# Five of sixteen expert pairs leave their outputs in DRAM, and the tokens fetch them by index

## The chip, the cores and the metric

The kernel runs on one core of a Trainium2 chip. The metric is device time in microseconds of one execution. TensorE multiplies matrices into PSUM, ScalarE and VectorE work element by element and read PSUM, GpSimd does small work and issues indirect DMAs, SyncE (SP) issues most loads. Each engine runs its instructions in order; DMAs issued from any of them are carried out by 16 DMA engines.

## The reference

One decoder layer on 512 tokens of width 1024, in float32: two attention branches (MLA and MoBA) merged by gates, an output projection, and then a mixture of experts and a final RMSNorm. The change touches the experts alone. In the reference they are

```python
g_sel = argmax(g_logits)                    # one of 4 groups
top_vals, top_idx = top_k(e_in, 2)          # two of the group's 8 experts
weight = p_group * softmax(top_vals)
...
(silu(xb @ w_g[e]) * (xb @ w_u[e])) @ w_d[e]        # e: 32 experts, D 1024, FF 256
out = zeros((T, D)).at[slot_tok].add(ys * slot_w[:, None])
```

Every token goes to two experts, so there are 1,024 choices over 32 experts, and each token's two expert outputs, weighted, are added to its row `x`.

## The kernel before, in words

Up to about 435 us the kernel computes the projections, the attention and the output projection, then the routing. What follows is the experts' stage, `experts()` (L819), which handles two experts at a time in 16 pairs, q = 0 to 15. A pair has 128 slots, one for each partition: 64 for each of its experts. A slot that holds no token has an index outside the tensor, and a gather skips it.

One pair runs so, in the order in which TensorE's instructions are written out (`tc.manual_schedule` for TensorE and GpSimd; the other engines' order is made by the framework's planner, but inside `last()` also by hand):

- `slot_weights` (L733): GpSimd copies the slot's routing weight and norm factor out of the gathered `wg` rows, in three small copies (L738 twice, L739).
- `gate_up` (L760): 32 matmuls G and 32 matmuls U (L769), then ScalarE's silu of G (L774) and VectorE's product with U (L775), both scaled by the norm factor.
- `some(5)`, `act_T`, `some(3)`: the combines of the pair before, with the transposes of the activations (L781) among them. `combine` (L811) adds one 128-token, 512-column block of the pair's outputs to the token rows `x2`: two matmuls (L815, L816) of a one-hot matrix S with the high and the low half of the outputs, and a VectorE add (L817). There are eight for each pair.
- `next_rows`: eight transposes (L746) of the next pair's gathered rows `xg`.
- `gather_rows` (L723) for pair q + 2: GpSimd issues two indirect DMAs (L728), of rows `xg` (4 KB each) and of rows `wg` (132 bytes each).
- `one_hot` (L806): VectorE makes S from the pair's token numbers.
- `down` (L786) for both halves of 512 columns: eight matmuls each (L795), then ScalarE writes the weighted high half (L802) and VectorE the low half (L803).

The weights of pair q + 2 are asked for at the beginning of pair q: six loads of 1 MB (two experts times gate, up and down), all on SP's queue. There are 20 buffers for them (`NH`). Each load also waits until the load before the previous one has landed (`load`, L678), so that two are in flight. The last pair's down weights come in four loads of half the size, by column halves, behind the load of `final_norm`.

After pair 15, `last()` (L876) computes the final norm and stores the output.

Of the kernel before, what the change touches and what calls it, by code (L numbers as in the profile page):

```python
# [10 lines left out]
F32 = mybir.dt.float32  # L11
# [3 lines left out]
I32 = mybir.dt.int32  # L15
U32 = mybir.dt.uint32
AF = mybir.ActivationFunctionType
ALU = mybir.AluOpType
# [3 lines left out]
P = 128  # L22
T = 512
NT = T // P
D = 1024
# [5 lines left out]
NEG = -1e30  # L31
NE = 32
NH = 20


class Layer:
# [351 lines left out]
    def attention(self, br, pairs):  # L388
# [4 lines left out]
        for m in pairs:  # L393
            O = self.op.tile([P, T], F32, name="O", tag="o")
            PT, Es = [], []
            for i in range(NT):
                n = (i + 1) * P
                qs = slice(i * P, n)
                S = both or [self.mp.tile([P, 512], F32, name="S", tag="m") for _ in range(2)]
                for h in range(2):  # L400
# [229 lines left out]
    def route_setup(self):  # L630
        nc, tc, io, c = self.nc, self.tc, self.io, self.const
        self.dram = dp = self.ctx.enter_context(tc.tile_pool(name="dram", bufs=1, space=bass.MemoryType.DRAM))
        self.x2d = dp.tile([T, D], F32, name="x2d")
        self.Wd = dp.tile([T, NE + 1], F32, name="Wd")
        self.wr = c.tile([P, KD, 40], F32, name="wr")
        nc.gpsimd.memset(self.wr, 0.0)
        self.load_late(self.wr[:, :, 0:4], io["w_router_group"][0].rearrange("(j p) g -> p j g", p=P))
        for g in range(4):
            self.load_late(self.wr[:, :, 8 + 8 * g:16 + 8 * g],
                              io["w_router_expert"][0, g].rearrange("(j p) e -> p j e", p=P))  # L640
        self.gpj = c.tile([P, KD], F32, name="gpj")
        self.load_late(self.gpj, io["ffn_norm"][0].rearrange("(p j) -> p j", p=P))
        self.gcol = gcol = c.tile([P, KD], F32, name="gcol")
        self.load_late(gcol, io["ffn_norm"][0].rearrange("(j p) -> p j", p=P))
        nc.vector.tensor_scalar(self.gpj, self.gpj, 32.0, None, ALU.mult)
        nc.vector.tensor_scalar(gcol, gcol, 32.0, None, ALU.mult)
        nc.vector.tensor_tensor(self.wr, self.wr, gcol.unsqueeze(2).to_broadcast([P, KD, 40]), ALU.mult)
        self.rb = c.tile([P, 40], F32, name="rb")
        nc.gpsimd.memset(self.rb, -3e38)
        self.load_late(self.rb[:, 0:4], io["b_router_group"][0:1, :].to_broadcast([P, 4]))  # L650
        self.load_late(self.rb[:, 8:40], io["b_router_expert"].rearrange("o g e -> o (g e)")
                          .to_broadcast([P, 32]))
        self.rc = c.tile([P, 33 + NT], F32, name="rc")
        self.load_late(self.rc, io["rconst"])
        self.iota32 = self.rc[:, 0:32]
        self.slot = self.rc[:, 32:33]
        self.token = self.rc[:, 33:33 + NT]
        self.tri = c.tile([P, 2, P], F16, name="tri")
        self.after(nc.gpsimd.dma_start(self.tri, io["tri"]), self.started)
        self.tm = c.tile([P, T], F16, name="tm")  # L660
        self.after(nc.gpsimd.dma_start(self.tm, io["tm"]), self.started)
        self.M = c.tile([P, NT, NE], F16, name="M")
        self.sq = c.tile([P, 2, NT], F32, name="sq")
        self.W = c.tile([P, NT, NE + 1], F32, name="W")
        self.iotaU = c.tile([P, NE], U32, name="iotaU")
        nc.vector.tensor_copy(self.iotaU, self.iota32)


    def new_w(self):
        i = self.nw % NH  # L670
        self.nw += 1
# [139 lines left out]
    def combine(self, S, y, half, t):  # L811
# [4 lines left out]
        nc.tensor.matmul(cp, S[:, t * P:(t + 1) * P], y[1], start=False, stop=True)  # L816
        nc.vector.tensor_tensor(self.x2[t][:, hs], self.x2[t][:, hs], cp, ALU.add)  # L817

    def experts(self):  # L819
        nc, tc = self.nc, self.tc  # L820
        NP = NE // 2
        wgu, wd = {}, {}
        for q in range(3):
            wgu[q], wd[q] = self.load_gu(q), self.load_d(q)
        self.yhl = self.wp.tile([P, 2048], F32R, name="yhl", tag="whi")
        with tc.manual_schedule(engines={mybir.EngineType.PE, mybir.EngineType.Pool}):
            xT, sw, xg = {0: self.xT0}, {}, {}
            S, y, todo = None, None, []
            for q in range(NP):
                if q > 0 and q + 2 < NP:  # L830
                    wgu[q + 2], wd[q + 2] = self.load_gu(q + 2), self.load_d(q + 2)
                    if q + 2 == NP - 1:
                        self.load_final()
                if q:
                    sw[q] = self.slot_weights(q, wg, nc.gpsimd)

                def some(n):
                    for _ in range(min(n, len(todo))):
                        self.combine(S, y[todo[0][0]], *todo[0])
                        todo.pop(0)  # L840

                def between(j):
                    if q == 0 and j == 3:
                        self.tokens()
                        xg[1] = self.gather_rows(self.xi[:, 1:2], self.rows)
                    if q == 0 and j == 5:
                        sw[0] = self.take_weights()
                    if q == 0 and j == 9:
                        self.count_blocks()
                a = self.gate_up(wgu.pop(q), xT.pop(q), lambda: sw[q][1], between)  # L850
                def next_rows():
                    xT[q + 1] = self.new_xT()
                    for g in range(2):
                        self.gathered_T(xg[q + 1][0], xT[q + 1], g)
                if q == 0:
                    next_rows()
                some(5)
                aT = self.act_T(*a)
                some(3)
                if 0 < q < NP - 1:  # L860
                    next_rows()
                if q + 1 < NP:
                    wg = xg.pop(q + 1)[1]
                if q + 2 < NP:
                    xg[q + 2] = self.gather_rows(self.xi[:, q + 2:q + 3])
                S = self.one_hot(self.xf[:, q:q + 1])
                dn = wd.pop(q)
                y = [None, None]
                todo = [(h, t) for h in range(2) for t in range(NT)]
                if q == NP - 1:  # L870
                    self.last(S, dn, aT, sw[q][0])
                    break
                for h in range(2):
                    y[h] = self.down(dn, aT, sw[q][0], h)
# [158 lines left out]
class Route:  # L1033
# [60 lines left out]
    def choose_experts(self):  # L1094
        nc, L = self.nc, self.L
        self.v8, vi = self.tmp("v8", [8]), self.tmp("vi", [8], U32)
        nc.vector.max(self.v8, self.es)
        nc.vector.max_index(vi, self.v8, self.es)
        self.Mk = self.tmp("Mk", [2, NE])
        nc.vector.tensor_tensor(self.Mk, L.iotaU.unsqueeze(1).to_broadcast([P, 2, NE]),  # L1100
                                vi[:, 0:2].unsqueeze(2).to_broadcast([P, 2, NE]), ALU.is_equal)
        nc.vector.tensor_tensor(L.M[:, self.t], self.Mk[:, 0], self.Mk[:, 1], ALU.add)
# [15 lines left out]

    def places(self):
        nc, L, t, N = self.nc, self.L, self.t, self.N  # L1120
        n = self.tmp("n", [2])
        for c in range(2):
            nc.vector.scalar_tensor_tensor(self.es, self.Mk[:, c], 1.0, N, ALU.mult, ALU.mult, accum_out=n[:, c:c + 1])
        self.at(self.AB[:, :, 0:64], n)
# [33 lines left out]
def shape_consts():  # L1158
    out = {}

    def tab(half):
        e = (-np.arange(half, dtype=np.float32) / np.float32(half)).astype(np.float32)
        inv = np.power(np.float32(500000.0), e).astype(np.float32)
        ang = np.arange(T, dtype=np.float32)[:, None] * inv[None, :]
        c, s = np.cos(ang).astype(np.float32), np.sin(ang).astype(np.float32)
        return [c, c, -s, s]
    out["rope"] = np.ascontiguousarray(np.concatenate(tab(16) + tab(8), axis=1))
    q = np.arange(P)[:, None]
    c = np.arange(T)[None, :]
    out["mask"] = np.where(c <= q + 384, np.float32(0), np.float32(NEG)).astype(np.float32)  # L1170
    tri = np.ones((P, 2, P), np.float32)
    tri[:, 0] = np.arange(P)[:, None] <= np.arange(P)[None, :]
    tri[:, 0] += 1024.0 * np.eye(P)
    out["tri"] = tri
    rc = np.zeros((P, 33 + NT), np.float32)
    rc[:, 0:32] = np.arange(32)
    rc[:, 32] = 1025 + np.arange(P) % 64
    rc[:, 33:] = np.arange(P)[:, None] + P * np.arange(NT)[None, :] - 1024
    out["rconst"] = rc
    out["tm"] = np.broadcast_to(np.arange(T, dtype=np.float32) - 1024, (P, T)).copy()  # L1180
    return out
# [30 lines left out]
```

## Time and profile before

| what | value |
|---|---|
| median of 3 runs | 706.75 us (706.09 to 708.14) |
| the profiled execution | 705.33 us |
| its span, first to last instruction | 703.5 us |
| TensorE busy | 683.6 us (97%) |
| VectorE busy | 398.8 us (57%) |
| ScalarE busy | 277.3 us (39%) |
| GpSimd busy | 70.9 us (10%) |
| moved by DMA | 148.17 MB, mean 211 GB/s |
| mean granted clock of TensorE | 0.992 |

Busy shares are averages over stages with different limits. Times of single instructions count from the span's start. TensorE's matmuls are pipelined and their ends are modelled, so what one costs is read from the distance between starts. A DMA's time to landing counts from its issue.

### The profile page before, as it was taken

The numbers are of one execution on the slowest core, as the hardware profiler recorded it, in microseconds if no ns is written. First come the engines' busy times: TensorE is split into PE (matmuls) and PEld (weight loads), VectorE is DVE, ScalarE is ACT, GpSimd is POOL, SyncE is SP. The second block draws the span as 40 slices with busy tenths as digits, with TensorE's granted clock in tenths as the row PEclk, the third lists the DMA queues.
The fourth block names the chain that finished last, engine by engine and source line by source line (L and its number), as shares of the span: only waits on it lengthen the run. The fifth ranks groups of instructions, "written<-read, shape, count | busy, mean of one in ns | idle before, by whom it ended". The sixth has DMA issues, their size and how long they took to land.

```text
span 703.5 us, 11377 instructions
## 1 busy us (share of the span) xinstructions
PE 683.6 (97%) x4262; PEld 522.5 (74%) x4262; DVE 398.8 (57%) x972; ACT 277.3 (39%) x623; POOL 70.9 (10%) x151
## 2 busy tenths in 40 slices
PE   8999999999999999999999999999999999999991
PEld 7998887777788888888888998566656666666651
DVE  5535956877829964423765317255555544555545
ACT  5747544555638663422333334211212111212123
POOL 1404000000000000000000012211121111111103
PEclk9999999999999999999999999999999999999996
DMA  8725431110272144212789758898999999999923
GB/s 256 152 61 90 106 121 60 61 49 13 68 171 61 27 156 119 61 61 94 262 301 352 287 189 315 316 361 308 377 364 393 392 394 355 372 377 348 367 89 122
DMA packets 73786, 148.17 MB, mean 211 GB/s; under 512 B 30938, under 2 KB 53554, under 8 KB 61952
## 3 DMA queue, kind: packets, MB, share of 16 engines
q1 hardware_dynamic: 67616, 138.69, 56.1%
q10 hardware_dynamic: 3040, 4.27, 2.3%
q0 software_dynamic: 3072, 4.46, 2.1%
q8 instruction: 35, 0.57, 0.3%
q14 instruction: 23, 0.19, 0.1%
HBM read 145.35 MB, written 4.26 MB: 213 GB/s over the span
## 4 chain that ended last, share of the span: by engine, by line
PE 88%; DMA 4%; issue 3%; DVE 2%; ACT 1%; POOL 1%; SPq 0%; POOLq 0%; DVEq 0%; ACTq 0%
PE yp L795 7%; PE G L769 6%; PE U L769 6%; PE pacc L96 5%; PE pacc L95 5%; PE pacc L94 5%; PE pacc L448 4%; PE pacc L447 4%; PE pacc L449 4%; PE cp L815 4%; PE cp L816 3%; PE ptr L420 3%; DMA wg<-Wd,xi 3%; PE S L402 2%; PE O L428 2%
## 5 line engine op out<-in xcount | busy, mean ns | idle before, releaser
L65 DVE SCALAR_TENSOR_TENSOR wlo<-wraw,ms,whi 128x256 fp32r<-128x256 f32 (+2 forms) x134 | 68.3, 552 | 31.4 <-ACT whi L64 31.2
L64 ACT ACTIVATE whi<-wraw,ms 128x256 fp32r<-128x256 f32 (+2 forms) x134 | 67.0, 559 | 42.1 <-PE pacc L448 20.1
L817 DVE TENSOR_TENSOR x<-x,cp 128x512 f32<-128x512 f32 x128 | 78.1, 682 | 0.8 <-PE cp L816 0.8
L94 PE MATMUL pacc<-whi,hThi 128*128 128x352 f32 (+1 forms) x192 | 72.6, 378 | 0.0
L95 PE MATMUL pacc<-wlo,hThi 128*128 128x352 f32 (+1 forms) x192 | 70.6, 369 | 0.0
L96 PE MATMUL pacc<-whi,hTlo 128*128 128x352 f32 (+1 forms) x192 | 70.5, 367 | 0.0
L775 DVE SCALAR_TENSOR_TENSOR a<-U,sw,a 128x256 f32<-128x256 f32 x16 | 11.0, 685 | 84.9 <-PE U L769 62.0
L795 PE MATMUL yp<-w,a 128*64 128x512 f32 x256 | 58.5, 598 | 0.5 <-ACT a L783 0.5
L769 PE MATMUL G<-w,xT 128*64 128x256 f32 x512 | 58.3, 380 | 0.0
L769 PE MATMUL U<-w,xT 128*64 128x256 f32 x512 | 58.2, 379 | 0.0
L769 PEld LDWEIGHTS G<-w,xT 128*64 128x64 f32 x512 | 36.5, 137 | 24.6 <-issue 4.6
L815 PE MATMUL cp<-yhl,S 128*128 128x512 f32 x128 | 53.6, 419 | 0.2 <-DVE x L817 0.2
L816 PE MATMUL cp<-yhl,S 128*128 128x512 f32 x128 | 50.8, 396 | 0.8 <-DVE yhl L803 0.8
L447 PE MATMUL pacc<-hThi,whi 128*128 128x512 f32 x128 | 50.6, 396 | 0.0
L448 PE MATMUL pacc<-hTlo,whi 128*128 128x512 f32 x128 | 50.4, 394 | 0.0
L769 PEld LDWEIGHTS U<-w,xT 128*64 128x64 f32 x512 | 36.7, 137 | 18.4
L449 PE MATMUL pacc<-hThi,wlo 128*128 128x512 f32 x128 | 50.1, 392 | 0.0
L415 ACT ACTIVATE E<-E,mx 128x128 f32<-128x128 f32 (+3 forms) x64 | 35.6, 557 | 20.5 <-DVE mx L412 19.7
L803 DVE SCALAR_TENSOR_TENSOR yhl<-yp,sw,yhl 128x512 fp32r<-128x512 f32 x32 | 24.0, 751 | 31.3 <-ACT yhl L802 31.3
L802 ACT ACTIVATE yhl<-yp,sw 128x512 fp32r<-128x512 f32 x32 | 22.0, 687 | 47.4 <-PE yp L795 47.4
L94 PEld LDWEIGHTS pacc<-whi,hThi 128*128 128x128 f32 x192 | 36.1, 188 | 5.2 <-issue 1.3
L95 PEld LDWEIGHTS pacc<-wlo,hThi 128*128 128x128 f32 x192 | 36.1, 188 | 4.5 <-issue 0.7
(221 smaller groups left out, 1307.8 us busy)
## 6 DMA issues: line engine op xcount, KB each, us to landing
w<-in_w_exp_gate_dram SPq DMA_DIRECT2D x32, 1024.0 KB, 6.1
w<-in_w_exp_up_dram SPq DMA_DIRECT2D x32, 1024.0 KB, 6.1
w<-in_w_exp_down_dram SPq DMA_DIRECT2D x30, 1024.0 KB, 5.8
wraw<-in_w_in_dram SPq DMA_DIRECT2D x14, 1024.0 KB, 5.3
wraw<-in_w_out_dram SPq DMA_DIRECT2D x4, 1024.0 KB, 7.1
wraw<-in_w_in_dram SPq DMA_DIRECT2D x5, 704.0 KB, 4.8
xs<-in_x_dram SPq DMA_DIRECT2D x4, 512.0 KB, 6.6
wraw<-in_w_o_mla_dram SPq DMA_DIRECT2D x4, 512.0 KB, 3.4
```

The source lines that it names most:

```text
L65: nc.vector.scalar_tensor_tensor(lo[:, k], raw[:, k], g, hi[:, k].bitcast(F32), ALU.mult, ALU.subtract)
L94: nc.tensor.matmul(ps[t][:, :ncols], act_hi[kk // 4][:, kk % 4, ts], hi[:, k], start=kk == 0, stop=False)
L95: nc.tensor.matmul(ps[t][:, :ncols], act_hi[kk // 4][:, kk % 4, ts], lo[:, k], start=False, stop=False)
L96: nc.tensor.matmul(ps[t][:, :ncols], act_lo[kk // 4][:, kk % 4, ts], hi[:, k], start=False, stop=kk == ktot - 1)
L447: nc.tensor.matmul(ps, hi[:, k, ds], self.hT[0][k // 4][:, k % 4], start=k == 0, stop=False)
L448: nc.tensor.matmul(ps, hi[:, k, ds], self.hT[1][k // 4][:, k % 4], start=False, stop=False)
L449: nc.tensor.matmul(ps, lo[:, k, ds], self.hT[0][k // 4][:, k % 4], start=False, stop=k == KD - 1)
L769: nc.tensor.matmul(GU[i][es, 0:256], xT[:, j, es], gu[e][i][:, j * 256:(j + 1) * 256], start=j == 0, stop=j == KD - 1)
L795: nc.tensor.matmul(yp[es], aT[:, j, es], wd[e][:, j * D + half * 512:j * D + half * 512 + 512], start=j == 0, stop=j == 1)
L815: nc.tensor.matmul(cp, S[:, t * P:(t + 1) * P], y[0], start=True, stop=False)
L816: nc.tensor.matmul(cp, S[:, t * P:(t + 1) * P], y[1], start=False, stop=True)
L817: nc.vector.tensor_tensor(self.x2[t][:, hs], self.x2[t][:, hs], cp, ALU.add)
```

## The change

`VIA` names five pairs. These make no one-hot matrix, no high and low halves and no combines. `down_out` scales the down products into a tile of 128 x 1024 on ScalarE, both halves, and ScalarE issues its store to 128 rows of a new DRAM tensor `yd` (640 rows). In pairs 11 to 14 `take_slots` is called twice for each block of 128 tokens, once for each of a token's two choices: GpSimd fills a tile with zeros, issues an indirect DMA that fetches one row of `yd` for each token (an index outside `yd`, where the choice was none of these ten experts, fetches nothing), and VectorE adds the tile to the token rows. The indices come from `slot_rows`, some 14 small VectorE operations in pair 1, out of the routing's masks `Mk` and slot numbers `place`, which are kept for it. For the pairs that still combine, the eight combines are done four in the next pair and four in the one after it, where q is from 1 to 10; from pair 11 on all eight are done in the next pair.

```diff
+VIA = (1, 3, 5, 7, 9)
...
+        self.yd = dp.tile([len(VIA) * P, D], F32, name="yd")
...
+    def slot_rows(self):
...
+        for t in range(NT):
+            for i in range(2):
+                nc.vector.scalar_tensor_tensor(junk, self.Mk[:, t, i], 1.0, self.base, ALU.mult, ALU.mult,
+                                               accum_out=rows[:, t, i:i + 1])
+        nc.vector.tensor_scalar(far, self.place, 1088.5, float(1 << 20), ALU.is_gt, ALU.mult)
+        nc.vector.tensor_tensor(rows, rows, self.place, ALU.add)
+        self.yi = c.tile([P, NT, 2], I32, name="yi")
+        nc.vector.tensor_tensor(self.yi, rows, far, ALU.add)
+
+    def down_out(self, wd, aT, sw, q):
+
+        nc = self.nc
+        y = self.bl.tile([P, D], F32, name="y", tag="yd", bufs=2)
+        for h in range(2):
+            nc.scalar.mul(y[:, h * 512:h * 512 + 512], self.down_products(wd, aT, h), sw)
+        i = VIA.index(q) * P
+        nc.scalar.dma_start(self.yd[i:i + P], y)
+
+    def take_slots(self, t, i):
+
+        nc = self.nc
+        y = self.bl.tile([P, D], F32, name="y", tag="yd", bufs=2)
+        nc.gpsimd.memset(y, 0.0)
+        nc.gpsimd.indirect_dma_start(out=y, out_offset=None, in_=self.yd,
+                                     in_offset=bass.IndirectOffsetOnAxis(ap=self.yi[:, t, i:i + 1], axis=0),
+                                     bounds_check=len(VIA) * P - 1, oob_is_err=False)
+        nc.vector.tensor_tensor(self.x2[t], self.x2[t], y, ALU.add)
...
-                some(5)
+                n = min(len(todo), 4) if VIA[0] <= q <= VIA[-1] + 1 else len(todo)
+                some((n + 1) // 2 + (n > 4))
                 aT = self.act_T(*a)
-                some(3)
+                some(n // 2 - (n > 4))
...
                 if q + 2 < NP:
                     xg[q + 2] = self.gather_rows(self.xi[:, q + 2:q + 3])
+                if q == 1:
+                    self.slot_rows()
+                if 0 <= q - VIA[-1] - 2 < NT:
+                    for i in range(2):
+                        self.take_slots(q - VIA[-1] - 2, i)
+                dn = wd.pop(q)
+                if q in VIA:
+                    self.down_out(dn, aT, sw[q][0], q)
+                    continue
                 S = self.one_hot(self.xf[:, q:q + 1])
-                dn = wd.pop(q)
```

## Rows read from the trace of the kernel before

**Rows 1.** The profile's page: busy time of TensorE; GB/s in 40 slices.
```profile
PE 683.6 (97%) x4262; PEld 522.5 (74%) x4262; DVE 398.8 (57%) x972; ACT 277.3 (39%) x623; POOL 70.9 (10%) x151
...
GB/s 256 152 61 90 106 121 60 61 49 13 68 171 61 27 156 119 61 61 94 262 301 352 287 189 315 316 361 308 377 364 393 392 394 355 372 377 348 367 89 122
```
**Rows 2.** Chain that ended last, in order of time: start, us, engine, tile, line.
```profile
544.77 3.45 PE G L769 x32
...
552.11 0.24 PE cp L816
552.58 0.23 PE cp L816
...
560.41 3.45 PE G L769 x32
...
670.03 3.45 PE G L769 x32
673.49 3.45 PE U L769 x32
...
681.09 3.58 PE yp L795 x16
...
693.30 1.30 DVE fin L922
```
**Rows 3.** Window 450 to 670 us: busy of five engines, clock, DMA share, GB/s.
```profile
450.00:670.00 220.00, 219.78 (x1488) 137.43 (x1486) 115.69 (x196) 43.27 (x84) 34.72 (x70) 1.00 0.96 366
```
**Rows 4.** SP's queue, 440 to 704 us: what it waited for, us, times, longest.
```profile
SPq L679 <- DMA w<-in_w_exp_up_dram: 72.2, 26, 5.2
...
SPq L679 <- PE G L769: 5.5, 3, 4.8
```
**Rows 5.** Timeline of SP: start, us to the second issue's end, pairs of loads.
```profile
453.52 3.59 SPq L679 DMA_DIRECT2D w<-in_w_exp_gate_dram  x2
...
539.57 2.83 SPq L679 DMA_DIRECT2D w<-in_w_exp_down_dram  x2
544.57 3.70 SPq L679 DMA_DIRECT2D w<-in_w_exp_gate_dram  x2
550.97 2.81 SPq L679 DMA_DIRECT2D w<-in_w_exp_up_dram  x2
...
651.30 2.82 SPq L679 DMA_DIRECT2D w<-in_w_exp_gate_dram  x2
```
**Rows 6.** The last up load and the last down load, each with its landing.
```profile
L679 SPq DMA_DIRECT2D w<-in_w_exp_up_dram x1: 328/328/328, 659.8 to 659.8; - x1
...
DMA to landing us min/median/max: 4.9/4.9/4.9
...
L679 SPq DMA_DIRECT2D w<-in_w_exp_down_dram x1: 545/545/545, 669.3 to 669.3; - x1
...
DMA to landing us min/median/max: 6.0/6.0/6.0
```
**Rows 7.** One line: GpSimd's fill of a tile of 128 x 1024.
```profile
L619 POOL MEMSET xg<- x1: 947/947/947, 429.3 to 429.3; 128x1024 f32 x1
```
**Rows 8.** DMA queues, 450 to 670 us: packets, MB, share of 16 engines.
```profile
q0 software_dynamic: 2333, 3.68, 4.8%
```
**Rows 9.** Timeline around the start of pair 11: start, us, what; idle before it and its releaser.
```profile
604.16 1.02 POOL L728 DMA_INDIRECT xg<-x2d,xi  x1 [6.02 <-PE ptr L746]
...
612.06 0.18 POOL L738 COPY sw<-wg 64x1 f32<-64x1 f32 x1 [5.34 <-DMA wg<-Wd,xi]
...
612.52 0.71 ACT L774 ACTIVATE a<-G,sw 128x256 f32<-128x256 f32 x1 [4.22 <-POOL sw L739]
614.51 0.69 DVE L775 SCALAR_TENSOR_TENSOR a<-U,sw,a 128x256 f32<-128x256 f32 x1 [5.43 <-PE U L769]
```
**Rows 10.** Windows of half a microsecond behind the last matmuls, columns as in rows 3.
```profile
689.50:690.00 0.50, 0.11 (x1) 0.00 (x0) 0.50 (x2) 0.50 (x2) 0.50 (x1) 1.00 0.00 0
...
692.00:692.50 0.50, 0.00 (x0) 0.00 (x0) 0.50 (x1) 0.50 (x2) 0.17 (x1) 0.79 0.00 0
```

More of the change, by code (lines that the diff above doesn't have):

```diff
@@ L652, in route_setup @@
                           .to_broadcast([P, 32]))
-        self.rc = c.tile([P, 33 + NT], F32, name="rc")
+        self.rc = c.tile([P, 33 + NT + NE], F32, name="rc")
         self.load_late(self.rc, io["rconst"])
@@ L657, in route_setup @@
         self.token = self.rc[:, 33:33 + NT]
+        self.base = self.rc[:, 33 + NT:]
         self.tri = c.tile([P, 2, P], F16, name="tri")
@@ L662, in route_setup @@
         self.M = c.tile([P, NT, NE], F16, name="M")
+        self.Mk = c.tile([P, NT, 2, NE], F32, name="Mk")
+        self.place = c.tile([P, NT, 2], F32, name="place")
         self.sq = c.tile([P, 2, NT], F32, name="sq")
@@ L817, in combine @@
         nc.vector.tensor_tensor(self.x2[t][:, hs], self.x2[t][:, hs], cp, ALU.add)
+    def slot_rows(self):
+        nc, c = self.nc, self.const
+        rows = c.tile([P, NT, 2], F32, name="yrows")
+        far = c.tile([P, NT, 2], F32, name="far")
+        junk = c.tile([P, NE], F32, name="yjunk")
+        for t in range(NT):
[21 more added lines that the diff above has]
+        nc.vector.tensor_tensor(self.x2[t], self.x2[t], y, ALU.add)
     def experts(self):
@@ L1098, in choose_experts @@
         nc.vector.max_index(vi, self.v8, self.es)
-        self.Mk = self.tmp("Mk", [2, NE])
+        self.Mk = L.Mk[:, self.t]
         nc.vector.tensor_tensor(self.Mk, L.iotaU.unsqueeze(1).to_broadcast([P, 2, NE]),
@@ L1120, in places @@
         nc, L, t, N = self.nc, self.L, self.t, self.N
-        n = self.tmp("n", [2])
+        n = L.place[:, t]
         for c in range(2):
@@ L1174, in shape_consts @@
     out["tri"] = tri
-    rc = np.zeros((P, 33 + NT), np.float32)
+    rc = np.zeros((P, 33 + NT + NE), np.float32)
     rc[:, 0:32] = np.arange(32)
     rc[:, 32] = 1025 + np.arange(P) % 64
-    rc[:, 33:] = np.arange(P)[:, None] + P * np.arange(NT)[None, :] - 1024
+    rc[:, 33 + NT:] = [64 * (2 * VIA.index(i // 2) + i % 2) - 1025 if i // 2 in VIA else 1 << 20 for i in range(NE)]
+    rc[:, 33:33 + NT] = np.arange(P)[:, None] + P * np.arange(NT)[None, :] - 1024
     out["rconst"] = rc
```

## The prediction

> **What bounds the kernel now.** I read the page's sums and slices first. TensorE is busy for 97% of the span, and in the slices from 492 us on the DMA engines move 350 to 390 GB/s as well [rows 1]. Two resources may be near their limit in the experts' stage, so the question is which one a saving reaches.
>
> The chain of waits in order of time answers for TensorE: from about 500 us on, a pair is gate products, up products, the eight combines of the pair before, the transposes of the next rows, and the down products, with nothing between them. One pair's gate products start at 544.77 and the next one's at 560.41, a period of 15.64 us [rows 2]. Taken alone, this says that each microsecond of matmul removed is a microsecond of kernel.
>
> The windows say otherwise. From 450 to 670 us the DMA share is 0.96 at 366 GB/s [rows 3]. SP's own waits in this stage are for earlier weight loads, 72.2 us for the up loads alone, and only 5.5 us for buffers held by gate products [rows 4]. So the weight stream is not held back by buffers that TensorE frees late; it is held back by its own two loads in flight. Its pace: the gate loads of pair 4 are issued at 453.52 and those of pair 15 at 651.30, 11 pairs in 197.78 us, 17.98 us a pair [rows 5]. TensorE takes 15.64. The stream loses 2.34 us on TensorE with every pair and lives on its head start.
>
> What is left of that head start in the last pair is the number that decides. The second up load of pair 15 is issued at 659.82 and lands 4.9 us later, at 664.7; the up products start at 673.49: 8.8 us. The last down load is issued at 669.33 and lands 6.0 us later, at 675.3; the down products start at 681.09 and their second half, which needs it, 1.79 us (half of 3.58) later, at 682.9: **7.6 us** [rows 2, 6]. A faster TensorE can therefore bring at most 7.6 us, and whatever the change adds to the stream before 675 us is taken off that first.
>
> **What the change removes from TensorE.** A combine is two matmuls; the starts at 552.11 and 552.58 give 0.47 us for one [rows 2], eight make 3.76, five pairs 18.8 us. The other pairs' eight are done as four and four, so each of pairs 1 to 10 becomes 1.88 us shorter, and 13.76 us is its new period. The gate products of pair 15, at 670.03 now, could start at 651.2. By that time their weights have not landed in the trace of before: the second gate load is issued 2.5 us after 651.30. TensorE passes the stream at about pair 10 or 11 and waits for it from there on. Nothing of the 18.8 us beyond the 7.6 can reach the end.
>
> **What it takes from and gives to ScalarE, VectorE and GpSimd.** ScalarE scales the same two halves as before and issues five more DMAs; VectorE loses five one-hots, ten low halves and 40 adds, and gains eight full-width adds, bounded by the final scaling of the same shape, 1.30 us each [rows 2], 10.4 us together, and some 14 small operations in pair 1. VectorE was busy 115.69 of 220 us [rows 3], so this costs nothing, unless an add that waits for its gather stands in front of the gated activations (below). GpSimd gets eight fills and eight gather issues in pairs 11 to 14, 0.95 us for a fill [rows 7] and about 1.3 for an issue with the gap behind it (1.02 and 0.3) [rows 9], 4.5 us a pair. The cover for this is TensorE's wait for loads; what it costs without that is the third rival.
>
> **What it adds to the DMA engines.** This is the term that I think decides.
> - Five stores of 128 x 1024 floats, 0.524 MB each, on ScalarE's queue. The nearest row is a weight load: with no gather in flight two loads of 1.049 MB are issued in 5.00 us (539.57 to 544.57), 2.5 us each [rows 5]. By bytes a store costs 1.25 us of the stream, 6.3 for five. The upper bound is a whole load's slot, 2.5 us, 12.5 together; the lower one is nothing, if it falls into idle DMA time. I take 6.3, because in the stretch around it the engines are busy.
> - Eight gathers of 128 indices. Empty places move nothing: in 450 to 670 us 13 gather pairs moved 3.68 MB, 0.283 MB a pair, where 128 rows of 4,096 and 132 bytes would be 0.54; that is 67 rows a pair [rows 8]. Ten of 32 experts then give some 335 rows, 1.37 MB, 0.17 MB a call. The lower bound is the queue's own busy share: 4.8% of 220 us, 10.6 us for 3.68 MB [rows 8], so 3.9 for 1.37. The upper bound is what the stream loses around a gather pair now: six loads at 2.5 us would be 15.0, they take 17.98, so 2.98 for two calls, 1.49 for one, 11.9 for eight; it is visible in place, since the two loads from 544.57, with a gather in flight, take 6.40 where those before took 5.00 [rows 5]. I take 0.79 a call, 6.3 together, nearer to the lower end, since no table of short rows comes with them.
>
> Sum: the stream ends 6.3 + 6.3 = 12.6 us later. (The bounds are 3.9 and 24.4.) Less the 7.6 of slack, the end moves by +5.0 us: 703.5 + 5.0 = 708.5 for the span. The profiled execution took 705.33, the median of the runs is 706.75; the same 5.0 on the median is **711.7 us**.
>
> The Trainium skill (Trainium Kernel Development and Optimization, Key Constraints) says that DMAs issued from SP's, ScalarE's and GpSimd's queues run on the same 16 DMA engines and interleave, so that a second queue saves only the time of issuing. By that rule the stores are not free for standing on ScalarE's queue. The trace agrees as far as it goes, in the 6.40 us beside a GpSimd gather [rows 5]. Its page DMA: Bandwidth & Descriptors (Specifications) puts a core's limit at HBM at about 358 GB/s; the loads without a gather run at 1.049 MB in 2.5 us, 419 GB/s [rows 5], so here the measurement decides. By the page's figure the 3.99 MB added would be an estimated 11.1 us and the end 3.5 us later.
>
> **Rivals.**
> - *Hidden transfers, so faster.* The DMA engines have 4% of 220 us free, 8.8 us [rows 3]. If the new transfers fall into these gaps, the delay is 12.6 - 8.8 = 3.8 us and the end 3.8 us earlier: 703 on the median. It decides for faster if the delay is under 5.5. For it: a store needs no completion before the next load. Against it: the gaps stand where a load that shared its engines with a gather lands late, and there the new bytes would stand in the same queue. Chance 0.15.
> - *The same delay, smaller.* Between 5.5 and 9.7 us it gives a change within 0.3% (2.1 us, about what a measurement here can tell from none): about 707. Chance 0.22.
> - *GpSimd in its order.* The second copy of the slot weights waits 5.34 us for the gathers issued just ahead of it, to 612.06; the gate's activation follows at 612.52 and VectorE's product, held by the up products, at 614.51 [rows 9]. If the copy waits for the new gathers too, it comes 4.5 us later in pairs 12 to 14; the product could then start at 612.52 + 4.5 + 0.71 = 617.7, 3.2 us late, 9.6 us of TensorE in three pairs. That hides behind the loads (TensorE gains 18.8 us) unless it falls on top of the waits for them; half of it doing so gives 716.5. Chance 0.08.
> - *The clock.* Waits of TensorE for loads should be 1 to 3 us a pair. Behind the last matmuls, which end 0.11 us into the slice from 689.5, the granted clock falls to 0.79 in the slice from 692.0, on the way to its lower level of 1.2 GHz [rows 10]. If the waits of the late pairs grow as long as that, the up and down products and combines after the last landing, 11.2 us [rows 2], take up to twice that: 723. Chance 0.05. The Trainium skill (TensorE: Matmul & The Clock Gate, Why this matters for your kernels) warns of idle gaps between bursts of matmuls for this reason; no gap between two bursts of this trace shows such a fall.
> - That the whole 18.8 us arrive, 688, would need the stream to run 11 us faster than now; no row speaks for it, and I give it no chance worth a number.
>
> **How the numbers follow.** My forecast, a stream delayed by 9.7 us or more, has 0.50 and a range of its own of 709 to 717. With the rivals: slower 0.50 + 0.08 + 0.05 = 0.63, within 0.3% 0.22, faster 0.15. The range reaches from the hidden transfers' 703 to 720 (a delay of 20.9 us); it leaves out the whole hiding of a cheaper gather below and most of the clock's case above.
>
> **What would show it.** Right: the gate products of pairs 2 to 10 about 13.8 us apart; from pair 10 or 11 on a wait of TensorE for a weight load in every pair; DMA share at 0.97 or more; the last down load landing near 688 instead of 675.3, and the down products of pair 15 ending right behind it. Wrong: the last load lands before 683 (the transfers were hidden, or cheaper than by bytes); TensorE in pairs 11 to 15 waits for slot weights or for a VectorE add rather than for a load; or the granted clock leaves 1.00 between 600 and 690.

## The result, and the profile after

| | before | after |
|---|---|---|
| median of the runs | 706.42 us (704.70 to 708.14) | 729.65 us (728.06 to 735.53) |
| ratio, 95% interval | 1 | 1.034 (1.028 to 1.041) |
| span of the profiled execution | 703.5 us | 726.3 us |
| mean granted clock | 0.992 | 0.979 |

The changed kernel is 23.2 us slower on the median and 22.8 us in the span. The forecast was +5.0. Where some of a kernel's executions lie more than 1.5% above its fastest, they are left out of the medians here and below. The lines of the experts have moved by 5 (the loads are L684, the gate and up products L774, the combines L820 and L821, their add L822); the store is L846, the fill L852, the gather L853, its add L856.

The page of the kernel after, beside [rows 1]: TensorE's share, the GB/s slices, and a line of the DMA issues (KB each, median us to landing).

```profile
PE 683.0 (94%) x4182; PEld 514.0 (71%) x4182; DVE 376.9 (52%) x944; ACT 277.4 (38%) x623; POOL 90.0 (12%) x167
...
GB/s 253 144 67 79 106 115 57 58 59 1 130 161 1 60 174 61 84 59 146 342 290 350 153 323 280 360 317 357 331 317 370 339 352 344 348 385 324 336 223 119
...
yd<-y ACTq DMA_DIRECT2D x5, 512.0 KB, 8.6
```

TensorE is busy for as long as before (683.0 and 683.6 us) with 80 matmuls fewer, and the slices of the experts' stage did not rise. The windows of the stage, columns as in [rows 3]:

```profile
450.00:670.00 220.00, 200.60 (x1328) 118.40 (x1326) 81.47 (x134) 41.47 (x80) 46.64 (x78) 0.97 0.94 346
...
570.00:590.00 20.00, 17.22 (x108) 9.91 (x110) 4.11 (x7) 3.08 (x6) 2.58 (x5) 0.91 0.94 352
590.00:610.00 20.00, 15.87 (x88) 8.89 (x86) 4.70 (x9) 2.39 (x5) 2.54 (x5) 0.83 0.95 358
```

More is to be moved, yet the DMA share falls from 0.96 to 0.94 and the rate from 366 to 346 GB/s: the transfers are not simply added to a full pipe. TensorE is idle for 19.4 of the 220 us, and its granted clock leaves 1.00.

TensorE's timeline shows where it starts to wait (gate products of pairs 1, 2, 8 and 9, then the up products of pair 10; in brackets idle time and releaser):

```profile
453.28 3.62 PE L774 MATMUL G<-w,xT 128*64 128x256 f32 x32
...
466.94 3.62 PE L774 MATMUL G<-w,xT 128*64 128x256 f32 x32
...
550.17 3.62 PE L774 MATMUL G<-w,xT 128*64 128x256 f32 x32
...
572.04 5.14 PE L774 MATMUL G<-w,xT 128*64 128x256 f32 x29 [3.70 <-DMA w<-in_w_exp_gate_dram]
...
597.43 6.62 PE L774 MATMUL U<-w,xT 128*64 128x256 f32 x30 [3.11 <-DMA w<-in_w_exp_up_dram]
```

The first pairs run 13.66 us apart. From pair 8 on the chain of waits, beside [rows 2], is made of weight loads to the end:

```profile
549.99 7.46 DMA w<-in_w_exp_up_dram
557.50 3.67 PE U L774 x30
564.15 7.84 DMA w<-in_w_exp_gate_dram
...
682.44 6.53 DMA w<-in_w_exp_gate_dram
689.04 6.66 DMA w<-in_w_exp_up_dram
695.74 3.67 PE U L774 x30
```

SP's waits, beside [rows 4], and SP's timeline, beside [rows 5]: the stream waits for its own loads, as before, and hardly for buffers.

```profile
SPq L684 <- DMA w<-in_w_exp_up_dram: 82.0, 26, 5.3
...
SPq L684 <- PE G L774: 5.2, 2, 4.8
```
```profile
457.96 2.80 SPq L684 DMA_DIRECT2D w<-in_w_exp_gate_dram  x2
...
679.99 2.77 SPq L684 DMA_DIRECT2D w<-in_w_exp_gate_dram  x2
...
699.86 0.55 SPq L684 DMA_DIRECT2D w<-in_w_exp_down_dram  x1
```

The last down load alone, beside [rows 6]:

```profile
DMA to landing us min/median/max: 5.8/5.8/5.8
```

The books close on these rows. The last down load lands at 699.86 + 5.8 = 705.7; it was 675.3 before, so the stream ends 30.4 us later. Less the 7.6 us of slack that is +22.8, which is the difference of the spans. The 30.4 are 4.4 of a later start (457.96 against 453.52), 24.3 between the gate loads of pair 4 and pair 15 (222.03 against 197.77 us), and 1.7 behind that. What remains to be found is what made the 24.3 and the 4.4.

Waits from 430 us on that touch the gathers:

```profile
POOL sw L743 <- DMA y<-yd,yi: 24.0, 4, 7.8
...
DVE x L856 <- DMA y<-yd,yi: 21.8, 6, 7.9
```

They are long, but TensorE waits for none of them here.

### The profile page after: what moved, and what is told of

The parts are those of the page before. It is cut to its first block, busy times and chain, and to the rows that moved or that the text cites. A ratio compares the mean times of both kernels' runs of the same rounds, so it can differ in the third digit from the quotient of the medians.

```text
span 726.3 us, 11091 instructions
## 1 busy us (share of the span) xinstructions
PE 683.0 (94%) x4182; PEld 514.0 (71%) x4182; DVE 376.9 (52%) x944; ACT 277.4 (38%) x623; POOL 90.0 (12%) x167
## 4 chain that ended last, share of the span: by engine, by line
PE 67%; DMA 22%; issue 5%; DVE 2%; ACT 1%; POOL 1%; SPq 0%; POOLq 0%; ACTq 0%; DVEq 0%
DMA w<-in_w_exp_up_dram 9%; DMA w<-in_w_exp_gate_dram 6%; DMA wg<-Wd,xi 5%; PE pacc L97 5%; PE pacc L96 5%; PE pacc L95 5%; PE U L774 5%; PE pacc L450 4%; PE pacc L449 4%; PE pacc L448 4%; PE ptr L421 3%; PE S L403 2%; PE O L429 2%; PE pacc L492 2%; PE pacc L494 2%
## 5 line engine op out<-in xcount | busy, mean ns | idle before, releaser
L774 PE MATMUL U<-w,xT 128*64 128x256 f32 x512 | 70.5, 414 | 18.4 <-DMA w<-in_w_exp_up_dram 18.3
L65 ACT ACTIVATE whi<-wraw,ms 128x256 fp32r<-128x256 f32 (+2 forms) x134 | 67.0, 560 | 43.0 <-PE pacc L449 20.6
L774 PEld LDWEIGHTS U<-w,xT 128*64 128x64 f32 x512 | 41.1, 149 | 44.4 <-DMA w<-in_w_exp_up_dram 22.4
L774 PE MATMUL G<-w,xT 128*64 128x256 f32 x512 | 61.9, 388 | 4.7 <-DMA w<-in_w_exp_gate_dram 4.7
L774 PEld LDWEIGHTS G<-w,xT 128*64 128x64 f32 x512 | 38.0, 140 | 31.4 <-issue 8.3
L822 DVE TENSOR_TENSOR x<-x,cp 128x512 f32<-128x512 f32 x88 | 54.1, 680 | 1.3 <-PE cp L821 1.3
L779 ACT ACTIVATE a<-G,sw 128x256 f32<-128x256 f32 x16 | 11.4, 712 | 88.5 <-POOL sw L744 60.6
L97 PEld LDWEIGHTS pacc<-whi,hTlo 128*128 128x128 f32 x192 | 36.2, 188 | 4.2 <-issue 0.2
L800 PEld LDWEIGHTS yp<-w,a 128*64 128x64 f32 x256 | 17.2, 136 | 30.4 <-issue 27.7
```

The lines of the kernel that those rows point to most:

```text
L65: nc.scalar.mul(hi[:, k], raw[:, k], g)
L97: nc.tensor.matmul(ps[t][:, :ncols], act_lo[kk // 4][:, kk % 4, ts], hi[:, k], start=False, stop=kk == ktot - 1)
L774: nc.tensor.matmul(GU[i][es, 0:256], xT[:, j, es], gu[e][i][:, j * 256:(j + 1) * 256], start=j == 0, stop=j == KD - 1)
L800: nc.tensor.matmul(yp[es], aT[:, j, es], wd[e][:, j * D + half * 512:j * D + half * 512 + 512], start=j == 0, stop=j == 1)
```

## The experiments

In the table "stretch" is the time on SP from the gate load of pair 4 to that of pair 15, from one profiled execution of each; the medians are of 4 to 10 executions of each kernel, but of two for the stores alone. Each ratio is to the kernel before as it ran beside that kernel: its medians were 706.0 to 706.4 us there, but 709.1 beside the five reads. Three kernels whose stream carries nothing added (before, the preparation alone, after without stores and gathers) have stretches of 197.8, 192.0 and 203.4 us, so a difference of two stretches holds to some 6 us, or about 1 us for each of five stores. Some expectations name stretches of 176.9, 188.8 and 220.8 us; counted from first gate load to first gate load, as for the kernel before, they are 176.7, 192.2 and 218.7.

| kernel | median us | ratio (95%) | stretch us |
|---|---|---|---|
| before | 706.4 | 1 | 197.8 |
| after | 729.65 | 1.034 (1.028 to 1.041) | 222.0 |
| after without stores and gathers | 703.7 | 0.994 (0.990 to 0.999) | 203.4 |
| after, stores alone | 717.8 | 1.017, unclear | 210.9 |
| after, gathers alone | 715.44 | 1.015 (1.008 to 1.022) | 204.2 |
| preparation alone | 710.05 | 1.006 (1.002 to 1.010) | 192.0 |
| before + 5 stores | 724.1 | 1.024 (1.019 to 1.029) | 218.7 |
| before + 5 reads | 717.23 | 1.011 (1.005 to 1.017) | 213.2 |
| before, three loads in flight | 708.15 | 1.002 (1.000 to 1.005) | 176.7 |
| the same + 5 stores | 709.6 | 1.003 (1.001 to 1.005) | 190.3 |
| after, three loads in flight | 717.25 | 1.015 (1.012 to 1.018) | 192.2 |
| the same, gathers early | 697.11 | 0.988 (0.983 to 0.993) | 189.2 |
| after, gathers early | 728.2 | 1.031 (1.027 to 1.035) | 226.0 |

**The change taken apart.** Without stores and gathers (five pairs' outputs are then missing):

```diff
-        i = VIA.index(q) * P
-        nc.scalar.dma_start(self.yd[i:i + P], y)
...
-                if 0 <= q - VIA[-1] - 2 < NT:
-                    for i in range(2):
-                        self.take_slots(q - VIA[-1] - 2, i)
```

> The changed kernel without the five stores and without the eight gathers and their adds: the combines of the five pairs are left out, and so is their part of the result. Theory (the weight stream decides, and the new transfers delay it): the stream runs at its old pace, about 18 us a pair, and the kernel gains what its slack was, 7.6 us, less some 3 us that the changed kernel was already late at the start of the experts: 699 to 703. Rival (the faster pace of TensorE, the halved combines or the new waits of VectorE and GpSimd cost the time, not the transfers): it stays at 715 or more.

Measured: 703.7 us, all runs from 699.3 to 714.4: just above the theory's range and far from the rival's. The stream did not keep its old pace, though: the stretch is 203.4 us. The stores alone (only the second part of the diff taken out):

> The changed kernel with the stores but without the eight gathers, fills and adds, so their part of the result is missing. In the trace of the changed kernel the gate loads of pairs 4 to 11 came 16.8 us further apart than before, and those of pairs 11 to 15 7.5 us. If the first part is the price of the stores (about 3 us each, more than my 1.25), this run is about 7 us below the changed kernel, 720 to 723, with a gate-to-gate stretch of pairs 4 to 15 near 214 us. Rival (stores cost their bytes, 1.25 us each, and the gathers carry the rest): 708 to 712.

Measured: four runs of 713.9, 721.8, 724.7 and 726.6, too far apart for a price; the median of the faster two, 717.8, lies between the two expectations. The one profiled was the fastest, so its stretch of 210.9 is the low end. The gathers alone (only the first part taken out; `yd` is filled with zeros early, so that the gathers have rows to fetch):

> The changed kernel with the gathers but without the stores in the experts; the rows that are fetched are filled with zeros early in the kernel, while the DMA engines are idle, so the five pairs add nothing to the result. If the stores are the dear part: 706 to 712, and the early stretch (gate loads of pairs 4 to 11) as long as before, about 126 us. Rival (the gathers are the dear part, or TensorE's faster pace): above 718.

Measured: 715.44, between the two expectations; but the filling delays the first gate products from 439.3 to 443.7 us and the gate load of pair 4 from 457.96 to 459.30, so that up to 4.4 us of it belong to this experiment and not to the gathers. The early stretch, pairs 4 to 11, is 128.2 us, near the 126 of the theory.

Taking the five stores out of the changed kernel saves 729.65 - 715.44 = 14.2 us, or up to 18.6 with the 4.4; adding them to the kernel with neither costs 717.8 - 703.7 = 14.1. That is 2.8 to 3.7 us a store where the forecast had 1.25; only in the fastest run of the stores alone it is less, 1.5 by the stretch ((210.9 - 203.4) / 5). The places agree. All five stores are issued between the gate loads of pairs 4 and 11: this part takes 142.6 us in the changed kernel, 128.2 with the gathers alone and 125.8 before, so 14 to 17 us fall where the stores stand. The gathers are issued from 629 us on, between the gate loads of pairs 11 and 15 or just behind: that part takes 79.4 us, 74.2 with the stores alone and 72.0 before, so 5 to 7 us, about what the forecast gave the gathers (6.3). The stores cost more than twice theirs.

**The preparation alone.** The changed kernel's tiles, index operations and tags, with the experts' pairs as before:

```diff
-                n = min(len(todo), 4) if VIA[0] <= q <= VIA[-1] + 1 else len(todo)
+                n = len(todo)
...
-                    self.down_out(dn, aT, sw[q][0], q)
-                    continue
+                    nc.vector.memset(self.bl.tile([P, D], F32, name="y", tag="yd", bufs=2)[:, 0:8], 0.0)
```

> The changed kernel's preparation (larger constants, the kept masks and places, the index arithmetic, room for the new tile) with the experts of the kernel before: all combines, no stores, no gathers. In the changed kernel's trace the experts begin 3.4 us late, though nothing before them was meant to change. If the preparation causes it, by where tiles lie in memory or by work in the routing: 709 to 711. If it was chance of an execution: 705 to 707.

Measured: 710.05, +3.6 us, with the first gate products at 439.2 as in the changed kernel (435.9 before). That the experts begin 3.3 us later is thus the preparation's, ahead of the experts, a term that the forecast did not have; what in it does so was not tried. And from here to the kernel with neither stores nor gathers, which takes the combines off TensorE, is 710.05 - 703.7 = 6.4 us: of 18.8 us saved on TensorE only a third arrives. That kernel, too, ends with its stream: its last down load lands at 683.6, and its span is 704.3, 20.7 behind, as it is 20.6 in the changed kernel (705.7 and 726.3).

**Stores by themselves.** First attempt, five stores of zeros (a tile of 128 x 1024) added to the kernel before:

> The kernel before, with nothing but five stores of 128 x 1024 zeros added, issued by ScalarE at the end of the down products of pairs 1, 3, 5, 7 and 9. Theory (a store costs the stream about 3 us wherever TensorE is): a stream delayed by some 14 us less the slack of 7.6, so 712 to 715. Rival (stores cost 1.25 us each, hidden in the slack): 705 to 708.

Measured: 706.16, but the stores ran at 256 to 263 us, long before the experts, since nothing tied them to a pair. It says nothing of the question. The second attempt ties each to its pair's last low part:

```diff
+                if q in (1, 3, 5, 7, 9):
+                    self.after(nc.scalar.dma_start(self.yd[q // 2 * P:q // 2 * P + P], z), self.low)
```

> The kernel before with five stores of 128 x 1024 zeros added, each tied behind VectorE's last write of the outputs of pairs 1, 3, 5, 7 and 9 (in the run e4 the planner had moved them to 256 us, so that it told nothing about this). Theory (a store costs the stream its bytes and a disturbance, about 3 us, whatever TensorE's pace): gate loads of pairs 4 to 15 about 211 us apart, time 712 to 715. Rival (1.25 us by bytes, so the five hide in the slack of 7.6): 204 us, and 705 to 708.

Measured: 724.1 and a stretch of 218.7, over both expectations. With TensorE's work unchanged, five stores cost 17.7 us on top of the slack: (17.7 + 7.6) / 5 = 5.1 us each; by the stretch it is (218.7 - 197.8) / 5 = 4.2. DMA queues of this kernel, 455 to 660 us (packets, MB, share of 16 engines; q1 is the weight stream, q10 the stores):

```profile
q1 hardware_dynamic: 8833, 64.28, 84.6%
...
q10 hardware_dynamic: 720, 2.62, 3.2%
```

and the weight stream of the kernel before in the same window:

```profile
q1 hardware_dynamic: 9849, 71.76, 90.7%
```

The stores' own packets take 3.2% of the engines' time, 1.3 us each, as the forecast had it. SP never waits for a store's landing here, but 2.62 MB stored have displaced 7.48 MB of loads: the stream's share fell by 6.1 points, nearly twice what the stores took, and each MB took 4% more of it on top (0.846 x 205 us / 64.28 MB = 2.70 us, against 2.59).

**Reads in place of stores**, the same bytes at the same places, from rows of the input into a tile that nobody reads:

```diff
+                    self.after(nc.scalar.dma_start(z, self.io["x"][0, 0:P, :]), self.low)
```

> The kernel before, two weight loads in flight, with five loads of 0.5 MB (rows of the input into a tile that nobody reads) on ScalarE's queue, each tied behind the pair's last low part where the run that took 724.1 us had a store of the same size: the same bytes at the same places, read in place of written. Theory that any second transfer costs a stream of two loads in flight 4 to 5 us, whichever way it goes: 718 to 726, and 215 to 222 us from the gate load of pair 4 to that of pair 15 (197.8 without, 220.8 with stores). Rival, that the price is that of writing among reads: a read costs its bytes, 1.25 us, five 6.3, of which the slack of 7.6 us hides all: 705 to 709, and 203 to 206 us for the stretch.

Measured: 717.23, between the two expectations. By the stretch a read costs (213.2 - 197.8) / 5 = 3.1 us, and by medians beside its own kernel before it is (717.23 - 709.1 + 7.6) / 5 = 3.1. So more than half of the price falls on any second transfer. That a store is dearer than a read shows in the times, whose intervals (1.019 to 1.029 and 1.005 to 1.017) do not meet; by the stretches alone, 4.2 against 3.1, it would not be clear.

**Three loads in flight.** In the kernel before, in the changed one, and in the kernel before with the tied stores, one line:

```diff
-        if len(self.loads) >= 2:
-            self.after(d, self.loads[-2])
+        if len(self.loads) >= 3:
+            self.after(d, self.loads[-3])
```

> The kernel before with three weight loads in flight instead of two, the control for the run with three in the changed kernel. TensorE sets its end, with 7.6 us of slack in the stream, so both theories expect the time of the kernel before within 2 us; theory A expects the stretch between the gate loads of pairs 4 and 15 to shrink below 190 us from 197.8, theory B within 3 us of it.

Measured: 708.15. The stretch shrinks from 197.8 to 176.7 us (16.1 a pair), and the time does not: the kernel before is bound by TensorE, and with two loads in flight its stream has only the 7.6 us to spare.

> The kernel before with five stores of 0.5 MB, each tied behind the pair's last low part as in the run that took 724.1 us, and with three weight loads in flight in place of two. Theory that a store is dear only because two loads leave the stream no reserve: the five stores cost their bytes, about 1.25 us each, which lie hidden behind TensorE: 707 to 711, and the stretch from the gate load of pair 4 to that of pair 15 takes 181 to 185 us, against 176.9 with three loads and no stores and 220.8 with two loads and stores. Rival, that a store is dear of itself (its queue holds up the others, or its packets slow theirs): 4 to 5 us each, a stretch of 195 to 202 us and 716 us or more.

Measured: 709.6, in the first theory's range and 14.5 us under the same stores with two loads in flight. The time cannot decide between the two, though: with three loads the stream is 21.1 us faster, and even five stores of 5 us would lie within that and the slack of 7.6. The stretch, 190.3, lies between the ranges; at 13.6 us over the 176.7 a store costs 2.7 us. By bytes, from 455 to 640 us, where both streams still have loads to issue, the stream moved 67.08 MB instead of 72.48, 5.40 less for the 2.62 stored; with two loads in flight it is 58.13 instead of 65.00, 6.87 less. So three loads lower the price, but not to the stores' bytes. SP's waits from 440 us on, and its issues around the last store, show what is left of it:

```profile
SPq L680 <- DMA yd<-z: 21.7, 3, 9.5
```
```profile
592.18 2.83 SPq L680 DMA_DIRECT2D w<-in_w_exp_up_dram  x2
604.57 0.81 SPq L680 DMA_DIRECT2D w<-in_w_exp_down_dram  x2
```

SP stands until a store has landed, at three of the five. Without stores a load follows the last one after 2.7 us on average (176.7 / 66); at these three places it follows after 5.6, 7.4 and 9.9, so by estimate some 15 us are added, as much as the whole 13.6. No line of the kernel asks for this wait. In the trace the load that waits is each time the next one to signal its landing on the semaphore (a counter that an instruction can wait for) that the store had used. With two loads in flight that semaphore comes round only 16 us or more after the store has landed, and SP's waits there name no store. The 4 to 5 us of a store there are thus not this wait, and with three loads hardly anything is left beside it.

> The changed kernel with three weight loads in flight instead of two. Theory A (the stream loses its time between loads: each new transfer makes one of the two in flight land late, and nothing stands behind it): the stretch between the gate loads of pairs 4 and 15 shrinks from 222 us towards the 200 us that the bytes need at the 380 GB/s of undisturbed stretches, and the kernel takes 700 to 712. Theory B (the engines are full, more in flight only share them): within 4 us of the changed kernel, 725 or more.

Measured: 717.25, between the two theories, 12.4 us under the changed kernel and 10.8 over the one before. The stretch is 192.2, 15.5 over its like without stores and gathers (176.7), where the changed kernel's is 24.3 over its own; the forecast had worked out 12.6 by bytes. SP waits for the landing of two stores here as well, 15.8 us in all. But another wait has come forward. Waits of this kernel from 430 us on:

```profile
DVE x L856 <- DMA y<-yd,yi: 26.2, 5, 8.5
POOL sw L743 <- DMA y<-yd,yi: 25.6, 4, 9.7
...
PE cp L820 <- DVE x L822: 19.5, 4, 8.0
```

and its chain of waits from 600 us on:

```profile
611.85 0.97 POOL y L852
613.09 1.00 POOL y L853
614.09 0.98 POOL y L852
615.33 10.76 DMA y<-yd,yi
626.24 1.22 POOL sw L743
...
641.23 9.24 DMA y<-yd,yi
650.67 1.16 POOL sw L743
...
665.37 6.56 DMA y<-yd,yi
```

GpSimd's copy of the slot weights and VectorE's add both wait for a gather issued just ahead of them; the adds of the combines queue behind on VectorE, and TensorE stands for 19.5 us in front of the combines.

**The gathers moved.** Three loads in flight, and fills and gathers at the start of pairs 11 to 14, behind the slot-weight copies, the adds tied behind the pair's last low part:

```diff
+                t = q - VIA[-1] - 2
+                ys = [self.take_slots(t, i) for i in range(2)] if 0 <= t < NT else []
...
-                if 0 <= q - VIA[-1] - 2 < NT:
-                    for i in range(2):
-                        self.take_slots(q - VIA[-1] - 2, i)
...
+                for v in ys:
+                    self.after(nc.vector.tensor_tensor(self.x2[t], self.x2[t], v, ALU.add), self.low)
```

> The changed kernel with three weight loads in flight, in which besides that the fills, the gathers of stored outputs and their additions are moved: the fills and gathers are issued at the start of pairs 11 to 14, behind the copies of the slots' weights, and the additions stand behind the pair's last low part on VectorE. With three loads in flight alone the kernel took 717.3 us, and TensorE stood about 8 us a pair in pairs 12 to 14 behind the slow additions. Theory that these waits are what is left between 717 and the gain on TensorE: they go, and what is left is the time before less the 18.8 us that TensorE saves, plus the preparation's 3.4, so 692 to 697, faster than both kernels. Rival, that GpSimd's copies still wait for the gathers, only elsewhere in the pair: 708 to 717, with the waits of about 8 us still on GpSimd's L743 and from there on the activation.

Measured: 697.11 us, 0.1 above the first theory's range and 1.2% faster than the kernel before. Its waits from 430 us on, and the window 450 to 640:

```profile
POOL sw L743 <- DMA y<-yd,yi: 5.0, 1, 5.0
...
PE cp L820 <- DVE x L822: 2.9, 3, 1.8
```
```profile
450.00:640.00 190.00, 185.66 (x1296) 110.75 (x1295) 77.53 (x128) 39.61 (x77) 44.55 (x77) 1.00 1.00 403
```

The 19.5 us are 2.9, and the engines carry 403 GB/s. The span is 9.5 us under that of before; 18.8 less 3.4 would be 15.4. TensorE is idle for 4.3 us of this window, which is most of what is missing; the rest was not placed.

The last run goes back to two loads in flight and keeps the move:

> The kernel of the 697.1 us run with two weight loads in flight again: of its two edits on the changed kernel only the move of the fills, gathers and additions is left. Theory that at two loads the weight stream sets the time and the waits for the gathered rows lie in its shadow: the move alone gains little, 720 to 731 beside 729.7 for the changed kernel, and the stretch from the gate load of pair 4 to that of pair 15 stays above 212 us (222.0 there, 188.8 with three loads). Rival, that the late additions cost the changed kernel time too: 19 of the 20 us between 717.2 and 697.1 come off at two loads as well, some 710.

Measured: 728.2, and a stretch of 226.0. With two loads the stream is the bound and the gathers' waits cost nothing; the move pays only once the stream is free. Neither edit alone beats the kernel before, both together do. The stretches of these two runs give the price of all stores and gathers: 226.0 - 197.8 = 28.2 us with two loads in flight, 189.2 - 176.7 = 12.5 with three.

## Why the prediction was wrong in its size

- *The mechanism* held. The weight stream decides, TensorE passes it and waits for loads, and the end moves by the stream's delay less 7.6 us of slack. The slack is confirmed by the landings: the span ends 20.6 us behind the half that needs the last load before (682.9 to 703.5), and 20.6 to 20.7 us behind that load's landing in the changed kernel and in the one without stores and gathers. The 6.4 us that the lighter TensorE brings with nothing added are no second measure of it, since the stretch of that run grew as well (203.4 against 197.8), which was not explained. TensorE's new period is 13.66 us where 13.76 was worked out. It passes the stream at pair 8 rather than 10 or 11, because the stream is slower than thought from the first store on.
- *The failed step* is the price of the stores: "By bytes a store costs 1.25 us of the stream". The stores' packets do take 1.3 us. Of the 30.4 us by which the stream ends later, where 12.6 were forecast, 16.8 lie between the gate loads of pairs 4 and 11, where the stores stand (6.3 forecast). A store costs 2.8 to 3.7 us in the changed kernel and 4.2 to 5.1 in the kernel before, over the upper bound of 2.5 as well (but for the one run at 1.5), since a whole load's slot was taken as the most that a store of half its size could displace. The row that could have warned was already there: two loads beside a gather took 6.40 us instead of 5.00 [rows 5].
- *Why bytes were the wrong unit* is shown in part. With two loads in flight 2.62 MB stored displace 6.87 MB loaded, and the DMA share falls; with three 5.40 MB, and there the stretch grows by no more than SP's waits for the stores' landings. The Trainium skill (Trainium Kernel Development and Optimization, Key Constraints) has the transfers of several queues interleave on the same engines. The runs agree, since ScalarE's stores slow SP's loads, and add that stores and gathers together lengthen the stretch by 28.2 us with two loads in flight and by 12.5 with three. By what path the bytes are lost with two was not shown.
- *The gathers*, 6.3 forecast: 5 to 7 us by the part of the stretch in which they stand.
- *A term left out*: the preparation, 3.3 us ahead of the experts. The forecast looked at pair 1's index operations and asked nothing of the stages before.
- *The rival of GpSimd's order* was right as a mechanism and hidden as said, behind the waits for loads. With the stream freed it cost TensorE 19.5 us; 9.6 had been worked out from GpSimd's copy alone; VectorE's adds, which wait for their gathers in front of the combines' adds, were not in that sum.
- *The clock.* It did leave 1.00: it was 0.83 between 590 and 610 us, where 30 up products took 6.62 us instead of 3.67, and 0.83 again between 670 and 690. The last pair's ran in 3.67, and SP waits for loads and not for buffers, so nothing suggests that it moved a load or set the end; no run was made without it.
- *Of the signs named*: the DMA share of 0.97 or more was wrong (0.94), which is the failed step seen from the other side; the last load was to land near 688 and landed at 705.7; the down products did end right behind it.

Not settled: why two loads in flight recover so badly from a disturbance, and how much of that a single execution shows by chance. The delay isn't local. In the changed kernel the six loads from 542.11 to 560.73 us, with the whole of a store among them (issued at 551.13), took 18.6 us, and the next six, to 580.16, with no store, 19.4; both are over the 17.98 of before.

## What to carry to other kernels

In a stream that keeps two transfers in flight near the engines' limit, price an added transfer not by its bytes but by what it displaces, here 3 to 5 us for 1.25 us of bytes. One more transfer in flight gave the stream 21 us of room and about halved that price here. Then read what the issuing queue waits for: SP stood for the landing of stores that no line of the kernel tied it to. When the bound is removed, ask at once which wait stood in its shadow; here one edit freed the stream and another freed the engines behind the new gathers, and only the two together gave 1.2%. And tie an added operation to the place that it is meant to be measured at, or it may run 200 us earlier. Before bytes are compared in a window, see that both streams still have something to load at its end.

## What the runs showed of the hardware

- With three loads of 1 MB in flight the stretch ran at 16.1 us a pair instead of 17.98, and the experts' stage reached 403 GB/s over 190 us. The Trainium skill (DMA: Bandwidth & Descriptors, Specifications) puts a core's limit at HBM at about 358 GB/s, half of what it gives for a stack that two cores share. This kernel runs on one core and exceeded that over a whole stage; the measurement decides.
- With two loads in flight, a load of 0.5 MB on a second queue cost the stream some 3.1 us, a store of the same size 4.2 to 5.1, of which the store's packets explain 1.3.
- In the changed kernel the granted clock fell between groups of matmuls that waited for loads: 0.91 between 570 and 590 us, 0.83 between 590 and 610, 1.00 from 610 to 650. Just ahead of the low stretch at 597 us TensorE had waited 3.11 us, and 30 matmuls then took 6.62 us instead of 3.67, 1.8 times as long, so most of them ran at the level of 1.2 GHz.
